# Strassen's seven products for the first two matrices of the second block's FFNs

## Chip, cores and metric

The kernel runs as one program on 1 core of one Trainium2 chip. The metric is device time in microseconds (us): the median of 3 runs of the kernel before is 2766.76 us (2765.35 to 2771.69).

## What is computed

The reference is a pair of two-layer transformer blocks on 256 tokens of width 1024, in float32. The change touches only the feed-forward networks (FFNs) of the second block. There are four of them: two layers `l`, two FFNs `f` in each.

```python
def swiglu_2(h, w_gate, w_up, w_down):
    return (jax.nn.silu(h @ w_gate) * (h @ w_up)) @ w_down

for l in range(DEPTH):                                   # DEPTH = 2
    h = rms_norm_2(x, norm_g[l, 0])
    x = x + 0.5 * swiglu_2(h, ffn_w_gate[l, 0], ffn_w_up[l, 0], ffn_w_down[l, 0])
    ...                                                  # attention
    h = rms_norm_2(x, norm_g[l, 2])
    x = x + 0.5 * swiglu_2(h, ffn_w_gate[l, 1], ffn_w_up[l, 1], ffn_w_down[l, 1])
```

Here `h` is 256 x 1024, `w_gate` and `w_up` are 1024 x 2816, and `w_down` is 2816 x 1024.

## The kernel before, in words

Every float32 operand is held as two parts, a rounded one (`h`, in tile `wh`) and what the rounding left out (`l`, in tile `wl`). `mm` (L432) multiplies two operands in three matmuls: high by high, high by low, low by high.

`Feed` (from L174) brings the weights. Its plan, made once by `all_weights` (L327), lists all weight blocks in the order in which TensorE uses them. `load` (L188) issues a 1 MB DMA on SP's queue for the next block (2048 columns of 128 partitions) as soon as a raw slot is free. `pump` (L202) splits the oldest raw block in pieces of 1024 columns: ScalarE copies the piece to `wh` with rounding (L220), and VectorE subtracts `wh` from the raw piece into `wl` (L221). Both of VectorE's inputs there lie in SBUF. At most `AHEAD` = 4 split pieces wait for TensorE. There are 3 raw and 3 split slots that all phases share, and 4 of each more while an FFN runs (`FFN_BUFS`). `take` (L231) hands a piece to TensorE's loop, `done` gives its slot back.

`ffn` (L560) goes over the 2816 middle columns in six chunks, five of 512 and one of 256. In a chunk `tokens` (L470) multiplies the tokens by the columns of `w_gate` (L610) and then by those of `w_up` (L611). Each has eight blocks of 128 rows and two tiles of 128 tokens, so 16 block products of three matmuls: 48 matmuls, 96 for both. ScalarE's Silu (L602) and VectorE's multiplication (L606) take the two results out of PSUM. Then `second` (L574) multiplies the chunk before by its rows of `w_down` (48 matmuls), TensorE transposes the chunk's result (L495), and ScalarE and VectorE split that as `gT` (L426, L427). Instructions run on each engine in the order in which they stand in its queue; GpSimd (POOL) has nearly nothing to do in the FFNs.

```python
            yield from self.tokens(xT, w1[:, f0:f0 + n], silu, ("lin", "lin"), ids)
            yield from self.tokens(xT, w3[:, f0:f0 + n], gate, ("tr" if nt == 2 else "lin", "lin"), ids)
            before = second(c - 1) if c else iter(())
```

Of the kernel before, what the change touches and what calls it, by code (L numbers as in the profile page):

```python
# [13 lines left out]
F32 = DT.float32  # L14
# [28 lines left out]
FFN_BUFS = (4, 4)  # L43
MOE_BUFS = (5, 4)
# [16 lines left out]
FFN_BANKS = {"acc": (0, 1, 2, 3), "lin": (4, 5), "tr": (6, 7)}  # L61
# [5 lines left out]
WIDE_CHUNKS = [(0, 512), (1024, 512), (2048, 384)]  # L67

# [84 lines left out]

class Feed:


    def __init__(self, nc, name):
        self.nc, self.name = nc, name
        self.free = ([], [])
        self.plan, self.raws, self.subs, self.plain = deque(), deque(), deque(), deque()  # L160
        self.live = deque()
        self.ahead = AHEAD
# [5 lines left out]
    def drop(self, phase):  # L168
# [19 lines left out]
    def load(self):  # L188

        if not self.plan:  # L190
            return False
        phase, src, k0, ks, split, heads = self.plan[0]
# [9 lines left out]
    def pump(self):  # L202
        nc = self.nc
        while True:
            moved = self.load()
            if self.raws and len(self.subs) < self.ahead:
# [3 lines left out]
                if slot:  # L210
# [13 lines left out]
                    if item[5] == kb:  # L224
                        self.raws.popleft()
                        self.free[0].append(rslot)
# [4 lines left out]
    def take(self, src):  # L231
# [3 lines left out]
        assert got.tensor.name == src.tensor.name and got.offset == src.offset and got.shape == src.shape  # L235
# [64 lines left out]
class Model:  # L300
# [28 lines left out]
    def all_weights(self):  # L329
        a, add = self.a, self.feed.add  # L330

        def ffn(phase, w1, w3, w2):
            n = len(FF_CHUNKS)
            down = lambda c: [w2[FF_CHUNKS[c][0]:sum(FF_CHUNKS[c]), :]]
            for c, (f0, m) in enumerate(FF_CHUNKS):
                add(phase, [w1[:, f0:f0 + m], w3[:, f0:f0 + m]])
# [95 lines left out]
    def mm(self, ps, lhs, rhs, start, stop):  # L432

        last = len(PASSES) - 1
        for i, (p, q) in enumerate(PASSES):
            self.nc.tensor.matmul(ps, lhs[p], rhs[q], start=start and i == 0, stop=stop and i == last)  # L436
# [123 lines left out]
    def ffn(self, pool, xT, w1, w3, w2, done, tiles=(0, 1), hook=None):  # L560
# [36 lines left out]
        for c, (f0, n) in enumerate(FF_CHUNKS):  # L597
# [12 lines left out]
            yield from self.tokens(xT, w1[:, f0:f0 + n], silu, ("lin", "lin"), ids)  # L610
            yield from self.tokens(xT, w3[:, f0:f0 + n], gate, ("tr" if nt == 2 else "lin", "lin"), ids)  # L611
# [1150 lines left out]
    def outer_norm(self, pool, gB):  # L1762

        nc = self.nc
        y = pool.tile([P, NT, D], F32, name="yout")
# [156 lines left out]
    def second_block(self):  # L1922
        nc, a = self.nc, self.a
        with self.tc.tile_pool(name="sb", bufs=1) as pool:
            half = lambda t, c0, n, ps: self.add_x(t, c0, n, ps, 0.5)
            col = lambda l, i: self.c1("norm_g_2", (l * 3 + i) * 8, 8)
            for l in range(L):
                for f in range(2):
                    with self.tc.tile_pool(name=f"f2_{l}{f}", bufs=1) as fp:
# [394 lines left out]
```

## Time and profile before

| | us |
|---|---|
| median of 3 runs (lowest, highest) | 2766.76 (2765.35, 2771.69) |
| the profiled execution's own time | 2769.47 |
| its span, first to last instruction | 2767.7 |
| TensorE busy in the span | 2708.2 |
| VectorE busy | 1909.6 |
| ScalarE busy | 1649.7 |
| GpSimd busy | 141.9 |
| first FFN of the second block, first matmul (1477.70) to the transposes after it (1663.77) | 186.07 |

The profile is of one execution. Busy time of TensorE includes the overlap of pipelined matmuls, so what a matmul costs is read from the distance between the starts of matmuls that follow each other and not from the length of one. The four FFNs lie at about 1478 to 1664, 1932 to 2115, 2122 to 2307 and 2576 to 2758 us of the span.

### The profile page before, as it was taken

What the parts mean: (1) busy time and instruction counts of PE and PEld (TensorE: products, weight loads), DVE (VectorE), ACT (ScalarE), POOL (GpSimd) and SP (SyncE); (2) the same over time, 40 slices, a digit from 0 to 9 for tenths busy, and PEclk for the clock granted to TensorE, in tenths of its full rate; (3) what the DMA queues carried; (4) which work ended last, traced back from release to release, by engine and by line L of the source; (5) the groups of instructions that cost most, each with busy time, mean ns of one, the idle gap of its engine ahead of it and who ended that gap; (6) DMA issues with size and microseconds to landing.
All of it is one profiled execution on the core that took longest, in us unless ns stands there. A gap on an engine that the chain in (4) does not pass through costs nothing. (4 is left out here: it accounts for less than half of the span.)

```text
span 2767.7 us, 38954 instructions
## 1 busy us (share of the span) xinstructions
PE 2708.2 (98%) x15206; PEld 2277.3 (82%) x15206; DVE 1909.6 (69%) x2618; ACT 1649.7 (60%) x2309; POOL 141.9 (5%) x183
## 2 busy tenths in 40 slices
PE   8999999999999999999989999999999999999998
PEld 7888888878888888888777888888888888988887
DVE  6565566668998998988876556776555446676554
ACT  6455455547887877777765446755444445674543
POOL 1220001310000000000000000010000000010000
PEclk9999999999999999999999999999999999999999
DMA  6327533337999999999966646446655546445651
GB/s 202 95 93 258 186 133 119 101 131 281 382 344 326 380 341 322 365 351 328 344 226 231 219 137 174 142 141 210 214 174 183 184 139 182 143 144 184 239 182 62
DMA packets 252646, 594.46 MB, mean 215 GB/s; under 512 B 26182, under 2 KB 62758, under 8 KB 252454
## 3 DMA queue, kind: packets, MB, share of 16 engines
q1 hardware_dynamic: 251206, 587.69, 61.1%
q0 software_dynamic: 1248, 4.20, 0.6%
q8 instruction: 122, 2.00, 0.3%
q14 instruction: 70, 0.57, 0.1%
HBM read 590.74 MB, written 1.10 MB: 214 GB/s over the span
## 5 line engine op out<-in xcount | busy, mean ns | idle before, releaser
L221 DVE TENSOR_TENSOR wl<-raw,wh 128x1024 fp32r<-128x1024 f32 (+2 forms) x1130 | 1314.3, 1186 | 596.9 <-ACT wh L220 583.6
L220 ACT ACTIVATE wh<-raw 128x1024 fp32r<-128x1024 f32 (+2 forms) x1130 | 1137.7, 1025 | 755.6 <-PE ps L436 708.1
L436 PE MATMUL ps<-wh,xT 128*128 128x512 f32 (+2 forms) x2944 | 919.2, 388 | 14.2 <-ACT xT L429 3.7
L436 PEld LDWEIGHTS ps<-wh,xT 128*128 128x128 f32 x2944 | 544.0, 190 | 136.7 <-DVE xT L430 7.5
L436 PE MATMUL ps<-wl,xT 128*128 128x512 f32 (+2 forms) x1472 | 563.9, 383 | 0.4 <-DVE wl L221 0.4
L436 PE MATMUL ps<-wh,gT 128*128 128x512 f32 x1584 | 500.3, 391 | 0.0
L436 PE MATMUL ps<-wh,xe 128*128 128x512 f32 (+1 forms) x1536 | 454.3, 373 | 0.0
L436 PEld LDWEIGHTS ps<-wh,gT 128*128 128x128 f32 x1584 | 297.3, 188 | 61.1
L436 PEld LDWEIGHTS ps<-wl,xT 128*128 128x128 f32 x1472 | 280.0, 190 | 53.8 <-DVE wl L221 2.1
L436 PEld LDWEIGHTS ps<-wh,xe 128*128 128x128 f32 x1536 | 284.5, 188 | 38.5
L436 PE MATMUL ps<-wl,gT 128*128 128x512 f32 x792 | 308.9, 391 | 0.9 <-DVE wl L221 0.8
L436 PE MATMUL ps<-wl,xe 128*128 128x512 f32 (+1 forms) x768 | 287.6, 375 | 2.7 <-DVE wl L221 2.4
L436 PE MATMUL ps<-xT,wh 128*128 128x256 f32 x960 | 177.9, 287 | 5.3 <-DVE z L845 2.7
L436 PEld LDWEIGHTS ps<-wl,gT 128*128 128x128 f32 x792 | 148.8, 188 | 32.6 <-DVE wl L221 2.3
L436 PEld LDWEIGHTS ps<-wl,xe 128*128 128x128 f32 x768 | 144.2, 188 | 27.3 <-DVE wl L221 7.0
L436 PEld LDWEIGHTS ps<-xT,wh 128*128 128x128 f32 x960 | 150.1, 192 | 7.8 <-ACT wh L220 2.8
L436 PE MATMUL ps<-xT,wl 128*128 128x256 f32 x480 | 135.8, 284 | 0.0
L436 PEld LDWEIGHTS ps<-xT,wl 128*128 128x128 f32 x480 | 92.0, 192 | 0.3 <-DVE wl L221 0.3
L1370 ACT ACTIVATE e<-e,mx 128x256 f32<-128x256 f32 (+1 forms) x160 | 76.0, 476 | 15.2 <-DVE mx L1368 14.8
L426 ACT ACTIVATE gT<-ps 128x512 fp32r<-128x512 f32 (+2 forms) x108 | 56.4, 553 | 30.1 <-PE ps L495 23.8
L503 ACT ACTIVATE junk<-x 128x512 bf16<-128x512 f32 x56 | 35.2, 628 | 63.3 <-DVE x L557 48.0
L427 DVE TENSOR_TENSOR gT<-ps,gT 128x512 fp32r<-128x512 f32 (+2 forms) x108 | 65.9, 639 | 0.6
(431 smaller groups left out, 2314.7 us busy)
## 6 DMA issues: line engine op xcount, KB each, us to landing
raw<-in_moe_w_dram SPq DMA_DIRECT2D x216, 1024.0 KB, 7.4
raw<-in_w_in_dram SPq DMA_DIRECT2D x50, 1024.0 KB, 5.2
raw<-in_moe_w_dram SPq DMA_DIRECT2D x64, 768.0 KB, 5.1
raw<-in_ffn_w_gate_dram SPq DMA_DIRECT2D x44, 1024.0 KB, 5.1
raw<-in_ffn_w_up_dram SPq DMA_DIRECT2D x44, 1024.0 KB, 5.5
raw<-in_ffn_w_down_dram SPq DMA_DIRECT2D x44, 1024.0 KB, 5.1
raw<-in_ffn_w_dram SPq DMA_DIRECT2D x33, 1024.0 KB, 5.2
raw<-in_w_gate_dram SPq DMA_DIRECT2D x24, 1024.0 KB, 5.1
```

What stands on the lines that cost most here:

```text
L220: nc.scalar.activation(ho, w, AF.Copy)
L221: nc.vector.tensor_tensor(lw, w, ho.bitcast(F32), op=ALU.subtract)
L426: nc.scalar.activation(h, src, AF.Copy)
L427: nc.vector.tensor_tensor(l, src, hf, op=ALU.subtract)
L436: self.nc.tensor.matmul(ps, lhs[p], rhs[q], start=start and i == 0, stop=stop and i == last)
L503: self.nc.scalar.activation(junk, self.x[:, t, h * 512:(h + 1) * 512], AF.Square, accum_out=ss[:, t, h:h + 1])
L1370: nc.scalar.activation(e[:, i], e[:, i], AF.Exp, bias=mx[:, i:i + 1], scale=-1.0, accum_out=sums[:, i:i + 1])
```

## The change

The two matrices of a chunk are seen as one 1024 x 1024 matrix of 2 x 2 blocks, each of 512 rows by 512 columns: `x1` and `x3` are the upper and the lower half of `w_gate`'s columns, `x0` and `x2` those of `w_up`'s. The tokens are 2 x 2 blocks too (128 tokens by 512 features). Strassen's scheme (in Winograd's form) makes the four results of seven block products instead of eight. For that four sums of weight blocks are needed (`t1` = x0 - x1, `t2` = x2 - t1, `t3` = x2 - x0, `t4` = x3 - t2), and four sums of token blocks, once for each FFN. The sums are made on GpSimd. It is done from the second chunk on; the first chunk is multiplied as before. A result now is a sum of products: three are added in PSUM, the others with copies (ScalarE) and additions (VectorE, and one on GpSimd).

```diff
+QUAD_BUFS = {(0, 0): (4, 4), (0, 1): (5, 4), (1, 0): (5, 4), (1, 1): (4, 4)}
-FFN_BANKS = {"acc": (0, 1, 2, 3), "lin": (4, 5), "tr": (6, 7)}
+FFN_BANKS = {"acc": (0, 1, 2, 3), "lin": (4, 5), "tr": (6, 7), "quad": (4, 5, 6, 7)}
...
+class Quad:
+    ORDER = ("x1", "t1", "t2", "x2", "t3", "x3", "t4")
+    LOADS = ("x1", "x0", "t1", "x2", "x3")
...
+    def sum(self, nc, out, a, b):
+        half = a.shape[1] // 2
+        for k in range(0, a.shape[1], half):
+            nc.gpsimd.tensor_tensor(out[:, k:k + half], a[:, k:k + half], b[:, k:k + half], op=ALU.subtract)
+
+    def derive(self, nc):
+        r = self.raw
+        if "t2" not in r and "x2" in r and "t1" in r and "x1" in self.split:
+            self.sum(nc, r["x1"], r["x2"], r["t1"])
+            r["t2"], self.slot["t2"] = r["x1"], self.slot["x1"]
+        elif "t3" not in r and "t2" in r:
+            self.sum(nc, r["x0"], r["x2"], r["x0"])
+            r["t3"], self.slot["t3"] = r["x0"], self.slot["x0"]
+        elif "t4" not in r and "t3" in r and "x3" in r and "t2" in self.split:
+            self.sum(nc, r["t2"], r["x3"], r["t2"])
+            r["t4"], self.slot["t4"] = r["t2"], self.slot["t2"]
...
+    def load_quad(self, phase, quad, name):
...
+        if name == "t1":
+            quad.sum(self.nc, raw, quad.raw["x0"], quad.raw["x1"])
+        else:
+            self.nc.sync.dma_start(raw, src.rearrange("(k p) n -> p k n", p=P))
...
+    def sums_T(self, pool, xT):
+        nc = self.nc
+        g = nc.gpsimd
+        full = [pool.tile([P, 4, S], F32, name=self.nm("full"), tag="gT0", bufs=2) for _ in range(2)]
+        for k, f in enumerate(full):
+            h, lo = [q[:, k * 4:k * 4 + 4, :].bitcast(F32) for q in xT.parts]
+            g.tensor_tensor(f, h, lo, op=ALU.add)
+        s = [pool.tile([P, 2, 4, P], F32, name=self.nm("sums"), tag="gT1", bufs=2) for _ in range(2)]
+        a = lambda t, k: full[k][:, :, t * P:(t + 1) * P]
+        g.tensor_tensor(s[0][:, 0], a(1, 0), a(1, 1), op=ALU.add)
+        g.tensor_tensor(s[0][:, 1], s[0][:, 0], a(0, 0), op=ALU.subtract)
+        g.tensor_tensor(s[1][:, 0], a(0, 0), a(1, 0), op=ALU.subtract)
+        g.tensor_tensor(s[1][:, 1], a(0, 1), s[0][:, 1], op=ALU.subtract)
+        parts = self.parts(pool, [P, 4, 4, P], "S")
+        for i in range(2):
+            self.put(parts, lambda q: q[:, 2 * i:2 * i + 2], s[i])
+        return parts
+
+    def quad(self, pool, quad, n, xT, sums, gs):
...
+        def gate(t):
+            g = (u2, u3)[t]
+            nc.vector.scalar_tensor_tensor(g, g, r[t], (p1, p5)[t], op0=ALU.mult, op1=ALU.mult)
+        def end_c11():
+            add(nc.vector, p1, C)
+            nc.scalar.activation(p1, p1, AF.Silu, scale=r[0])
+            gate(0)
+        def end_c22():
+            copy(u3, A)
+            nc.gpsimd.tensor_tensor(u3, u3, p5, op=ALU.add)
+        def end_c21():
+            nc.scalar.activation(p5, A, AF.Silu, scale=r[1])
+            gate(1)
...
+        plan = [
+            ("x1", A, xT.parts, own(0, 0), True, lambda: copy(p1, A)),
+            ("t1", B, sums, mixed(0), True, lambda: copy(p5, B)),
+            ("t2", A, sums, mixed(1), False, lambda: copy(u2, A)),
+            ("x2", B, sums, mixed(3), False, lambda: add(nc.vector, u2, B)),
+            ("t3", A, sums, mixed(2), False, end_c22),
+            ("x3", C, xT.parts, own(0, 4), True, end_c11),
+            ("t4", A, xT.parts, own(1, 4), False, end_c21),
+        ]
...
-            yield from self.tokens(xT, w1[:, f0:f0 + n], silu, ("lin", "lin"), ids)
-            yield from self.tokens(xT, w3[:, f0:f0 + n], gate, ("tr" if nt == 2 else "lin", "lin"), ids)
+            if c in quads:
+                yield from self.quad(pool, quads[c], n, xT, sums, gs)
+            else:
+                yield from self.tokens(xT, w1[:, f0:f0 + n], silu, ("lin", "lin"), ids)
+                if quads:
+                    sums = self.sums_T(pool, xT)
+                yield from self.tokens(xT, w3[:, f0:f0 + n], gate, ("tr" if nt == 2 else "lin", "lin"), ids)
```

How this moves instructions is seen in two places. The first is VectorE's queue in a middle chunk of the last FFN. Here is the kernel before, from a chunk's multiplications (L606) to the split of `gT` (L427); names with the same stem and another number are other buffers (`ps` lies in PSUM, all else in SBUF):

```order
L606 SCALAR_TENSOR_TENSOR g_27429<-ps_27365,rs_26922,sa_27355 128x512
L606 SCALAR_TENSOR_TENSOR g_27431<-ps_27366,rs_26922,sa_27357 128x512
L221 TENSOR_TENSOR wl_27434<-raw_27167,wh_27433 128x1024
L221 TENSOR_TENSOR wl_27452<-raw_27205,wh_27451 128x1024
L221 TENSOR_TENSOR wl_27468<-raw_27205,wh_27467 128x1024
L221 TENSOR_TENSOR wl_27486<-raw_27239,wh_27485 128x1024
L221 TENSOR_TENSOR wl_27518<-raw_27239,wh_27517 128x1024
L427 TENSOR_TENSOR gT_27502<-ps_27503,gT_27501 128x4x128
L427 TENSOR_TENSOR gT_27502<-ps_27510,gT_27501 128x4x128
```

In the changed kernel this is the stretch of a chunk that adds up the results (L302 is L221 of before, L681 the additions, L685 the multiplications, L519 is L427):

```order
L681 TENSOR_TENSOR g_27506<-ps_27502,g_27506 128x512
L302 TENSOR_TENSOR wl_27602<-raw_27297,wh_27601 128x1024
L302 TENSOR_TENSOR wl_27614<-raw_27280,wh_27613 128x1024
L302 TENSOR_TENSOR wl_27626<-raw_27280,wh_27625 128x1024
L302 TENSOR_TENSOR wl_27638<-raw_27359,wh_27637 128x1024
L681 TENSOR_TENSOR sa_27504<-ps_27503,sa_27504 128x512
L302 TENSOR_TENSOR wl_27651<-raw_27359,wh_27650 128x1024
L302 TENSOR_TENSOR wl_27663<-raw_27413,wh_27662 128x1024
L685 SCALAR_TENSOR_TENSOR g_27506<-g_27506,rs_27352,sa_27504 128x512
L685 SCALAR_TENSOR_TENSOR g_27507<-g_27507,rs_27352,sa_27505 128x512
```

A chunk of 512 columns had 12 splits on VectorE and now has 18, two additions out of PSUM are new, and the two multiplications now read both inputs from SBUF. The second place is GpSimd's queue, which had nothing in the chunks of an FFN. In the changed kernel one period of it, in the last FFN, is this (L174 are the halves of the weight sums, L694 is the addition of `end_c22`):

```order
L174 TENSOR_TENSOR raw_27581<-raw_27558,raw_27512 128x1024 x2
L694 TENSOR_TENSOR g_27507<-g_27507,sa_27505 128x512
L174 TENSOR_TENSOR raw_27558<-raw_27605,raw_27558 128x1024 x2
L174 TENSOR_TENSOR raw_27512<-raw_27605,raw_27581 128x1024 x2
L174 TENSOR_TENSOR raw_27512<-raw_27629,raw_27512 128x1024 x2
L174 TENSOR_TENSOR raw_27840<-raw_27817,raw_27771 128x1024 x2
```

The rows are `t1` of the next chunk, the addition for this chunk, then `t3`, `t2` and `t4` of the next, and `t1` of the one after: eight subtractions of 1024 columns for a chunk, and the addition ahead of three of the next chunk's sums.

## Rows read from the trace of the kernel before

**Rows 1.** The page: busy time by engine, the chain that ended last.

```profile
PE 2708.2 (98%) x15206; PEld 2277.3 (82%) x15206; DVE 1909.6 (69%) x2618; ACT 1649.7 (60%) x2309; POOL 141.9 (5%) x183
...
PE 36%; issue 7%; DVE 1%; DMA 1%; ACT 1%; ACTq 0%; POOLq 0%; POOL 0%; SPq 0%; DVEq 0%
```

**Rows 2.** Busy time by stretch: one middle chunk, first and last FFN.

```profile
core 0: us, PE busy (x) PEld busy (x) DVE busy (x) ACT busy (x) POOL busy (x), PEclk, DMA share, GB/s
...
1566.00:1600.00 34.00, 34.00 (x153) 27.75 (x152) 17.08 (x17) 14.96 (x16) 0.00 (x0) 1.00 0.55 187
...
1481.00:1666.00 185.00, 184.33 (x855) 150.93 (x855) 101.37 (x107) 84.04 (x98) 1.71 (x3) 0.98 0.58 198
...
2576.00:2761.00 185.00, 182.76 (x859) 150.68 (x857) 94.44 (x98) 81.06 (x95) 0.94 (x2) 1.00 0.46 158
```

**Rows 3.** Timeline of TensorE, first FFN: start, us, engine, line, operation, tiles, count.

```profile
1533.30 0.39 PE L436 MATMUL ps<-wl,xT 128*128 128x512 f32 x1
...
1554.99 0.40 PE L436 MATMUL ps<-wl,xT 128*128 128x512 f32 x1
...
1567.47 0.39 PE L436 MATMUL ps<-wl,xT 128*128 128x512 f32 x1
...
1635.69 0.28 PE L436 MATMUL ps<-wl,xT 128*128 128x256 f32 x1
...
1646.69 0.28 PE L436 MATMUL ps<-wl,xT 128*128 128x256 f32 x1
...
1646.92 0.40 PE L436 MATMUL ps<-wh,gT 128*128 128x512 f32 x1
...
1663.77 1.04 PE L535 MATMUL ps<-ident,x 128*128 128x128 f32 x8
```

**Rows 4.** Groups by form, VectorE, 1532 to 1634 us (count, busy, mean ns).

```profile
L221 DVE TENSOR_TENSOR wl<-raw,wh 128x1024 fp32r<-128x1024 f32 x36 | 44.1, 1226 | 48.4 <-ACT wh L220 48.3
L606 DVE SCALAR_TENSOR_TENSOR g<-ps,both,sa 128x512 f32<-128x512 f32 x6 | 4.2, 744 | 0.0
L427 DVE TENSOR_TENSOR gT<-ps,gT 128x512 fp32r<-128x512 f32 x6 | 3.8, 683 | 0.0
```

**Rows 5.** Groups by form, ScalarE, 1532 to 1634 us.

```profile
L220 ACT ACTIVATE wh<-raw 128x1024 fp32r<-128x1024 f32 x36 | 38.2, 1060 | 54.5 <-PE ps L436 52.7 <-DVE T L1889 1.7
L602 ACT ACTIVATE sa<-ps,both 128x512 f32<-128x512 f32 x6 | 4.1, 689 | 3.1 <-PE ps L436 3.1
L426 ACT ACTIVATE gT<-ps 128x512 fp32r<-128x512 f32 x6 | 3.2, 584 | 0.0
```

**Rows 6.** Groups by form, GpSimd, whole span.

```profile
L2215 POOL TENSOR_TENSOR y<-od,subg 128x512 f32<-128x512 f32 x4 | 5.2, 1297 | 0.3
...
L733 POOL TENSOR_TENSOR rp<-qraw,sincos 128x64 f32<-128x64 f32 x4 | 1.3, 318 | 0.0
```

**Rows 7.** Timelines of GpSimd and VectorE, attention, 1859 to 1872 us.

```profile
1860.95 2.55 POOL L2126 TENSOR_TENSOR merged<-merged,gate 128x512 f32<-128x512 f32 x2 [6.33 <-DVE gate L2125]
1867.61 3.53 POOL L2126 TENSOR_TENSOR merged<-merged,gate 128x512 f32<-128x512 f32 x2 [4.10 <-DVE gate L2125]
...
1861.29 0.69 DVE L2125 TENSOR_TENSOR gate<-ps,gate 128x512 f32<-128x512 f32 x1 [0.43 <-PE ps L436]
1862.44 2.14 DVE L221 TENSOR_TENSOR wl<-raw,wh 128x1024 fp32r<-128x1024 f32 x1 [0.46 <-ACT wh L220]
...
1868.43 1.55 DVE L221 TENSOR_TENSOR wl<-raw,wh 128x1024 fp32r<-128x1024 f32 x1 [0.30 <-ACT wh L220]
1870.90 1.32 DVE L221 TENSOR_TENSOR wl<-raw,wh 128x1024 fp32r<-128x1024 f32 x1 [0.92 <-ACT wh L220]
```

**Rows 8.** Granted clock (PEclk) around a stop of TensorE, first FFN's start.

```profile
1478.00:1488.00 10.00, 9.61 (x20) 5.40 (x19) 6.13 (x11) 7.31 (x11) 0.69 (x1) 0.51 0.98 340
1488.00:1498.00 10.00, 10.00 (x44) 8.03 (x43) 4.58 (x5) 3.18 (x3) 0.00 (x0) 0.98 0.94 340
...
1477.70 0.87 PE L436 MATMUL ps<-wh,xT 128*128 128x512 f32 x2 [1.81 <-ACT wh L220]
```

More of the change, by code (lines that the diff above doesn't have):

```diff
@@ L151, in backwards, with __init__, release @@
     return bass.AP(tensor=ap.tensor, offset=ap.offset + step * (n - 1), ap=dims)
+class Quad:
+    ORDER = ("x1", "t1", "t2", "x2", "t3", "x3", "t4")
+    LOADS = ("x1", "x0", "t1", "x2", "x3")
+    def __init__(self, w1, w3):
+        self.src = {"x1": w1[0:512, :], "x0": w3[0:512, :], "x3": w1[512:1024, :], "x2": w3[512:1024, :]}
+        self.raw, self.slot, self.split, self.gone = {}, {}, set(), set()
+    def sum(self, nc, out, a, b):
[14 more added lines that the diff above has]
+        else:
+            return False
+        return True
+    def release(self):
+        r, s = self.raw, self.split
+        over = {"t1": "t1" in s and "t2" in r, "x2": "x2" in s and "t3" in r, "t3": "t3" in s,
+                "x3": "x3" in s and "t4" in r, "t4": "t4" in s}
+        new = [n for n, o in over.items() if o and n not in self.gone]
+        self.gone.update(new)
+        return [self.slot[n] for n in new]
 class Feed:
@@ L205, in pump @@
             moved = self.load()
-            if self.raws and len(self.subs) < self.ahead:
+            for quad in self.quads:
+                moved |= quad.derive(nc)
+                self.free[0].extend(quad.release())
+            if self.quads and len(self.quads[0].split) == 7:
+                self.quads.pop(0)
+            if self.raws and self.raws[0][0] is None:
+                quad, n = self.raws[0][3]
+                self.raws[0][0] = quad.raw.get(n)
+            if self.raws and self.raws[0][0] is not None and len(self.subs) < self.ahead:
                 item = self.raws[0]
@@ L430, in put, with mm @@
             nc.vector.scalar_tensor_tensor(l, src, scale, hf, op0=ALU.mult, op1=ALU.subtract)
-    def mm(self, ps, lhs, rhs, start, stop):
+    def mm(self, ps, lhs, rhs, start, stop, reopens=False):
         last = len(PASSES) - 1
         for i, (p, q) in enumerate(PASSES):
-            self.nc.tensor.matmul(ps, lhs[p], rhs[q], start=start and i == 0, stop=stop and i == last)
+            self.nc.tensor.matmul(ps, lhs[p], rhs[q], start=start and i == 0, stop=stop and i == last,
+                                  skip_group_check=reopens)
     def mul(self, xT, sub, targets, last):
@@ L562, in ffn @@
+    def ffn(self, pool, xT, w1, w3, w2, done, tiles=(0, 1), hook=None, quads={}):
         nc = self.nc
```

68 lines of the change are left out of this document (60 added, 8 removed).

## The prediction

> **What bounds the kernel now.** I read the page first: TensorE is busy for 2708 of 2767.7 us and heads the chain that ended last, no other engine has over 69% [rows 1]. Then the stretches: in a middle chunk of an FFN TensorE works all 34 of 34 us, VectorE 17, ScalarE 15, GpSimd 0, at a granted clock of 1.00, and the first and the last FFN look the same (184 and 183 of 185 us) [rows 2]. So TensorE sets the pace there, and a matmul taken away is worth the distance between two starts. A chunk's first product steps from 1533.30 to 1554.99 in 31 groups of three matmuls, 0.70 us a group or 0.233 each; a whole chunk takes 1567.47 - 1533.30 = 34.17 us; in the last chunk, 256 columns wide, 31 groups take 1635.69 to 1646.69, 0.355 a group [rows 3]. But the change gives VectorE and GpSimd work in return, and the view to read next is what those two do to each other. That is seen only in the attention, where GpSimd works: a split on VectorE that takes 1.23 us by itself [rows 4] took 2.14 when it began inside two GpSimd multiplications, and it ended at 1864.58, 1.08 us after they did (1860.95 + 2.55 = 1863.50). In the next pair a split that began at 1868.43 took 1.55, and GpSimd's two instructions, 2.55 in the pair before, took 3.53: the second stood still until the split had ended (1869.98), and ended 1.16 us after that. A multiplication of VectorE that reads PSUM (1861.29) lies within GpSimd's work and takes its usual 0.69 [rows 7]. I read this as: an instruction of VectorE with two inputs in SBUF and one of GpSimd with two inputs in SBUF never run together; the one that comes later waits for the whole of the other. All splits are of the first kind, all new sums of the second.
>
> **What goes.** In a chunk 84 matmuls stand for 96, 12 fewer: 12 x 0.233 = 2.8 us in each of 16 full chunks, 12 x 0.118 = 1.4 in each of 4 last ones: 44.8 + 5.7 = 50.5 us of TensorE. A full chunk is then worth 34.17 - 2.8 = 31.4 us of TensorE.
>
> **What comes.** (1) Splits. A product has its own weights of 2048 columns, so a chunk has 7 x 2 = 14 pieces for 8, and with those of `w_down` 18 for 12. ScalarE: 6 x 1.06 us more, with four copies out of PSUM at about 0.69 some 9 us a chunk; it was idle for 54.5 of 102 us [rows 5], 18 us a chunk, which covers it. VectorE: 18 x 1.08, where 1.08 is what a split needs behind GpSimd [rows 7], makes 19.4 us. (2) The two multiplications now have both inputs in SBUF; at half a split's width I take 0.6 each, 1.2. (3) Two additions out of PSUM, and the two splits of `gT` that were there: 4 x 0.68 = 2.7 us by the nearest row (L427) [rows 4], beside which GpSimd may run. (4) GpSimd's eight subtractions of 1024 columns. No row has this width. Instructions with 512 columns take 1.297 and with 64 take 0.318 [rows 6], so a column costs 2.19 ns and 512 more cost 1.12: with the 1.16 of a queued one [rows 7] that gives 2.28; twice a lone one, 2.59, is the other bound. I take 2.3, by the row it is nearest to, since these will be queued: 8 x 2.3 = 18.4, and 1.2 for the addition: 19.6 us. The Trainium skill (GPSIMD Engine Reference, section 3.1) gives 4497 ns for an addition of 2048 columns, so 18.0 in place of 18.4; no run here shows that width.
>
> So a full chunk needs the excluded pair for 19.4 + 1.2 + 19.6 = 40.2 us, against 31.4 on TensorE and 34.2 before. **The work that hid VectorE is no longer enough cover**, and TensorE will wait for weights. It can't be evened out by working ahead, since only four pieces may be split ahead and `t4` waits for the split of `t2`.
>
> **The sum for one FFN.** VectorE: 8 splits of the first chunk, 56 + 7 of the products, 22 of `w_down`, 2 for the token sums = 95 x 1.08 = 102.6; multiplications 8 x 0.6 + 2 x 0.3 = 5.4. GpSimd: 32 subtractions and 2 token additions at 2.3 = 78.2; 8 narrow subtractions, 4 token sums and 4 additions at 1.16 = 18.6; 0.6 for the last addition. Together 205.4 us, of which 4 splits (4.3) are done before the FFN begins. Behind the last product's split TensorE still has that product (1.4) and `w_down`, 1663.77 - 1646.92 = 16.9 [rows 3], in which 6 splits and two multiplications (7.1) go on. So 205.4 - 4.3 + 18.3 - 7.1 = 212.3 us against 186.07, 26 more; four times, 105. Of VectorE's instructions that read PSUM (10 additions, 12 splits of `gT`, some 14 us an FFN) GpSimd's work covers a part; none to all is possible, and I count a third, 4.7, as added: 19 in all. 2769.5 + 105 + 19 = 2893 for the profiled execution; the median stands 2.7 us below it: **2890 us**, 4.5% slower.
>
> The bounds: with all of those covered and ten us more done ahead in each FFN, 4 x 16 = 64, 2831; with none covered and 2.59 for a subtraction (34 x 0.29 = 10 an FFN), 4 x (26 + 14 + 10) = 200, 2967.
>
> Edits at no cost: the DMAs carry the same bytes (eight more on SP's queue, from halving the last chunk's), at a busy share of 0.46 to 0.58 [rows 2]; were they late, raw slots would be the cause, of which the sum `t1` now holds one. The output tile shares a buffer with the token sums, which are long done by then. PSUM's four rotating banks can hold TensorE at a chunk's start until `gT` is split; the wait for weights is longer.
>
> **Rivals.** *Faster, the exclusion doesn't bite* (0.13). VectorE is idle for 48.4 of 102 us in the middle chunks, nearly all of it waiting for ScalarE [rows 4]; were the sums to fall in that time, TensorE would stay the bound and 50.5 us would be won, some 5 given back at the FFNs' starts: 2722. The deciding point is a subtraction's price: with 20.6 for VectorE and 1.2 for the addition, 31.4 leaves 9.6 us for eight, 1.2 each. Rows 6 have that for half the width, and [rows 7] show no overlap at all, in both orders.
>
> *A smaller loss* (0.12). The first chunk, the products with `w_down` and the gaps between phases take up more than I grant: 8 us an FFN, 2800.
>
> *Worse: stops of TensorE lower its clock* (0.11). At the first FFN's start TensorE stopped for 1.81 us, and in the 10 us from 1478 it was granted 0.51, the 1.2 GHz level, and did 20 matmuls where the next 10 us did 44 [rows 8]. A split that waits 2.3 us for GpSimd is such a stop. GpSimd's addition is one more: it waits for `t3`'s product and holds the next chunk's sums behind it. One stretch like that in each of 20 chunks, at 5 us, is 100: 2990. Against it, a slow TensorE lets the splits catch up. The Trainium skill (TensorE: Matmul & The Clock Gate, section "What's actually happening") calls the throttled state the default, released by activity; by that rule a TensorE busy for three quarters could lose its clock again and again; the trace agrees for this one stop, and no run here shows a long stretch at that share.
>
> *Nothing measurable* (0.02). The change does do what it says, 20 x 12 = 240 matmuls are gone from the queue, so gain and loss would have to cancel.
>
> **How the numbers follow.** The forecast has 0.62, and with the two other slow cases slower by over 0.2% (what a measurement of this kernel can tell from no change) has 0.85, within 0.2% 0.02, faster 0.13. The range leaves out the fast case, no change and the outer parts of the two slow rivals: 2790 to 3000.
>
> **What would show it.** Right: in the middle chunks TensorE is busy for about three quarters, with idle time ended by L302 (`wl`); splits have a mean well over 1.23 us and GpSimd's subtractions well over 2.3, because both contain waits; a chunk takes 40 to 43 us. Wrong: splits stay at 1.23 beside GpSimd's work, or a subtraction takes near 1.2 us, and a chunk takes 31 to 32 us; or TensorE's clock falls in the chunks, and the loss is nearer to 220 us.

## The result and the profile after

The changed kernel takes 2947.56 us (median of 4 runs, 2944.71 to 2950.75), the kernel before beside it 2767.71 (4 runs, 2765.35 to 2771.69): a ratio of 1.0649 with a 95% interval of 1.0630 to 1.0667, 180 us slower. The forecast was 2890, with a range of 2790 to 3000 and 0.85 for slower.

The page of the changed kernel, with the rows that answer to [rows 1] (busy time of each engine, the chain that ended last):

```profile
PE 2712.0 (92%) x14966; PEld 2240.0 (76%) x14966; DVE 2317.9 (79%) x2774; ACT 1797.8 (61%) x2505; POOL 680.6 (23%) x387
...
PE 25%; DVE 12%; issue 6%; POOL 3%; ACT 2%; DMA 2%; SPq 0%; ACTq 0%; POOLq 0%; DVEq 0%
```

The 240 matmuls are gone (15206 to 14966), yet TensorE was busy no less (2708.2 to 2712.0). VectorE rose by 408 us and now stands in the chain with 12% instead of 1%; GpSimd rose from 142 to 681.

Where in the program? A chunk ends with the transposes of its result (L588), so their starts mark the chunks. The timeline of TensorE in the second FFN (start, us, engine, line, operation):

```profile
2041.74 1.03 PE L588 MATMUL ps<-ident,g 128*128 128x128 f32 x8
...
2085.84 1.04 PE L588 MATMUL ps<-ident,g 128*128 128x128 f32 x8
```

From one to the next is 44.1 us. The table was made in this way for both kernels from their timelines; "to the first" is the distance from the last transposes of the FFN before (for the first FFN, of the phase before) to the first of this one, so it holds all that lies between, the start and the ordinary first chunk.

| FFN | before: to the first, then chunks 2 to 6 | after | more |
|---|---|---|---|
| 1 | 90.3; 33.7 34.2 34.2 34.2 17.7 | 97.7; 44.0 43.9 44.2 39.1 17.3 | 41.9 |
| 2 | 296.9; 33.8 34.3 34.3 34.3 17.7 | 308.1; 42.1 44.1 47.3 38.2 16.3 | 44.8 |
| 3 | 37.8; 33.9 34.3 34.3 34.3 17.7 | 48.4; 41.9 44.3 47.6 38.1 16.3 | 44.3 |
| 4 | 296.9; 33.8 34.3 34.3 34.3 17.7 | 312.0; 39.0 45.1 45.5 39.1 17.3 | 46.7 |

The four sums make 177.7 us, so the loss lies in these FFNs: 44 us in the four stretches to the first transposes (7.4 + 11.2 + 10.6 + 15.1) and 133 in the chunks. Chunks 2 to 4 take 39 to 48 us, chunk 5 some 38 to 39, and the half chunk is a little faster than before.

Busy time by stretch, changed kernel: three full chunks of the second FFN and its half chunk (columns as in [rows 2]).

```profile
1999.67:2041.74 42.07, 32.69 (x138) 24.73 (x139) 40.91 (x25) 21.89 (x25) 25.42 (x10) 1.00 0.45 150
2041.74:2085.84 44.10, 33.74 (x141) 24.91 (x140) 40.54 (x25) 22.70 (x26) 26.16 (x10) 1.00 0.43 143
2085.84:2133.14 47.30, 34.84 (x141) 26.26 (x140) 40.47 (x25) 22.72 (x26) 26.30 (x10) 0.96 0.36 122
...
2171.39:2187.73 16.34, 16.34 (x117) 15.32 (x116) 15.83 (x16) 12.53 (x18) 5.21 (x3) 1.00 0.22 68
```

In a full chunk VectorE shows 40 to 41 us of work and GpSimd 26, together 66 in 42 to 47: both counts hold the time for which an instruction stands blocked by the other engine. TensorE has 33 to 35, three quarters. In the half chunk TensorE is busy throughout.

Groups by form, changed kernel: VectorE from 1990 to 2450 us, then GpSimd over the whole span (count, busy, mean ns, idle before).

```profile
L302 DVE TENSOR_TENSOR wl<-raw,wh 128x1024 fp32r<-128x1024 f32 x186 | 341.7, 1878 | 37.5 <-ACT wh L301 37.1
```

```profile
L174 POOL TENSOR_TENSOR raw<-raw,raw 128x1024 f32<-128x1024 f32 x128 | 392.8, 3084 | 236.8 <-DVE wl L302 219.0 <-DMA raw<-in_ffn_w_up_dram 17.9
```

A split has a mean of 1878 ns, where it had 1226 [rows 4], with the same form and line of code. VectorE's idle time behind ScalarE, 48.4 us of 102 before, is 37.5 of 460.

What TensorE waited for, changed kernel, from 1485 us to the end (total us, times, longest):

```profile
PE ps L528 <- DVE wl L302: 127.1, 106, 4.1
PE ps L528 <- DVE gT L519: 22.2, 8, 4.0
PE ps L528 <- ACT wh L301: 18.1, 3, 7.1
```

In the kernel before, from 1479 us on, the same view has this row for `wl` (L221) and none for the other two:

```profile
PE ps L436 <- DVE wl L221: 0.4, 1, 0.4
```

So 167.4 us of new stops stand against 50.5 us saved, 117 net. And TensorE's busy time, 3.8 us more with 50.5 us of matmuls fewer, says that the others took some 54 longer. The clock is about half of that: the mean granted clock is 0.982 over 2942.9 us and was 0.991 over 2767.7, so 53.0 and 24.9 us of full speed are missing, 28 more.

One of those stops, in the fourth FFN, shows how the pieces hang together. The timeline of GpSimd, of VectorE and of TensorE, changed kernel (in brackets the idle time before and what ended it):

```profile
2832.30 2.41 POOL L174 TENSOR_TENSOR raw<-raw,raw 128x1024 f32<-128x1024 f32 x1 [8.43 <-DVE wl L302]
2835.87 3.32 POOL L174 TENSOR_TENSOR raw<-raw,raw 128x1024 f32<-128x1024 f32 x1 [1.16 <-DVE wl L302]
```

```profile
2819.20 2.47 DVE L302 TENSOR_TENSOR wl<-raw,wh 128x1024 fp32r<-128x1024 f32 x1 [0.87 <-ACT wh L301]
2821.87 3.08 DVE L302 TENSOR_TENSOR wl<-raw,wh 128x1024 fp32r<-128x1024 f32 x1 [0.20 <-ACT wh L301]
2824.87 1.27 DVE L519 TENSOR_TENSOR gT<-ps,gT 128x512 fp32r<-128x512 f32 x2
2831.00 1.22 DVE L302 TENSOR_TENSOR wl<-raw,wh 128x1024 fp32r<-128x1024 f32 x1 [4.85 <-ACT wh L301]
2833.33 10.35 DVE L302 TENSOR_TENSOR wl<-raw,wh 128x1024 fp32r<-128x1024 f32 x6 [1.11 <-ACT wh L301]
```

```profile
2825.60 0.79 PE L528 MATMUL ps<-wh,S 128*128 128x512 f32 x1 [3.99 <-DVE gT L519]
```

The split that began at 2821.87 stands behind GpSimd and takes 3.08 us instead of 1.2. Behind it in VectorE's order is the split of `gT` (L519), which frees the PSUM bank that the next product's result is to use; TensorE stops for 3.99 us. The windows around it:

```profile
2820.00:2823.00 3.00, 1.62 (x12) 1.21 (x10) 2.80 (x2) 2.03 (x3) 3.00 (x2) 1.00 0.14 57
2823.00:2831.00 8.00, 5.40 (x13) 4.28 (x14) 3.15 (x4) 1.06 (x1) 0.87 (x1) 0.57 0.43 133
2831.00:2838.00 7.00, 6.51 (x29) 5.03 (x28) 5.89 (x4) 5.57 (x8) 4.54 (x2) 1.00 0.00 0
```

The second window begins inside the stop; its mean clock is 0.57, and it has 13 matmuls where the next 7 us have 29. Here are the 5 us right behind this stop, then the start of the matmul behind the next stop for `gT`, one of 3.63 us, and the 5 us behind that:

```profile
2825.60:2830.60 5.00, 5.00 (x12) 3.93 (x13) 0.55 (x1) 0.69 (x1) 0.00 (x0) 0.50 0.69 213
...
2873.59 0.50 PE L528 MATMUL ps<-wh,S 128*128 128x512 f32 x1 [3.63 <-DVE gT L519]
...
2873.59:2878.59 5.00, 5.00 (x22) 4.16 (x23) 4.43 (x3) 3.02 (x4) 3.85 (x2) 1.00 0.33 101
```

Behind the first TensorE is granted 0.50, the 1.2 GHz level, and does 12 matmuls; behind the second 1.00, and it does 22. Of the eight stops for `gT` (3.98, 3.07, 2.99, 0.83, 2.96, 0.78, 3.99 and 3.63 us, in order of time) five have 0.50 to 0.66 in the 5 us behind them; the two short ones and the last have 1.00. So the length of a stop alone does not tell whether the clock falls. From 2823 to 2831 VectorE works 3.15 of 8 us and GpSimd 0.87: GpSimd's next sum waited 8.43 us for a split, and the split for ScalarE. That time, unlike a stop for a split, is lost to the excluded pair too.

### The profile page after: what moved, and what is told of

Same layout as the page of the kernel before. It is cut to its first block, busy times and chain, and to the rows that moved or that the text cites. A ratio compares the mean times of both kernels' runs of the same rounds, so it can differ in the third digit from the quotient of the medians.

```text
span 2942.9 us, 39264 instructions
## 1 busy us (share of the span) xinstructions
PE 2712.0 (92%) x14966; PEld 2240.0 (76%) x14966; DVE 2317.9 (79%) x2774; ACT 1797.8 (61%) x2505; POOL 680.6 (23%) x387
## 4 chain that ended last, share of the span: by engine, by line
PE 25%; DVE 12%; issue 6%; POOL 3%; ACT 2%; DMA 2%; SPq 0%; ACTq 0%; POOLq 0%; DVEq 0%
PE ps L528 22%; DVE wl L302 10%; POOL raw L174 2%; ACT wh L301 1%; PE ps L2267 1%; PE ps L588 1%; DMA raw<-in_ffn_w_up_dram 1%; PE ps L1546 1%; DMA narows<-rpbscr 1%; PE ps L2433 0%; POOL full L660 0%; DVE g L685 0%; PE ps L2170 0%; DMA raw<-in_ffn_w_gate_dram 0%; PE ps L2173 0%
## 5 line engine op out<-in xcount | busy, mean ns | idle before, releaser
L302 DVE TENSOR_TENSOR wl<-raw,wh 128x1024 fp32r<-128x1024 f32 (+3 forms) x1238 | 1666.6, 1379 | 344.1 <-ACT wh L301 328.0
L301 ACT ACTIVATE wh<-raw 128x1024 fp32r<-128x1024 f32 (+3 forms) x1238 | 1244.7, 1027 | 673.4 <-PE ps L528 604.5
L528 PE MATMUL ps<-wh,xT 128*128 128x512 f32 (+2 forms) x2144 | 703.8, 399 | 38.2 <-ACT wh L301 20.0
L174 POOL TENSOR_TENSOR raw<-raw,raw 128x1024 f32<-128x1024 f32 (+1 forms) x160 | 457.9, 2877 | 287.0 <-DVE wl L302 258.1
L528 PEld LDWEIGHTS ps<-wh,xT 128*128 128x128 f32 x2144 | 407.1, 194 | 136.1 <-ACT wh L301 21.7
L528 PE MATMUL ps<-wl,xT 128*128 128x512 f32 (+2 forms) x1072 | 426.6, 398 | 58.7 <-DVE wl L302 58.5
L528 PEld LDWEIGHTS ps<-wl,xT 128*128 128x128 f32 x1072 | 208.1, 194 | 118.0 <-DVE wl L302 82.1
L528 PE MATMUL ps<-wh,S 128*128 128x512 f32 (+1 forms) x640 | 193.2, 380 | 19.9 <-DVE gT L519 18.2
L528 PE MATMUL ps<-wl,S 128*128 128x512 f32 (+1 forms) x320 | 125.3, 392 | 49.8 <-DVE wl L302 49.7
L528 PEld LDWEIGHTS ps<-wh,S 128*128 128x128 f32 x640 | 119.2, 193 | 44.1 <-DVE gT L519 20.7
```

The costliest lines, as they stand in the source:

```text
L174: nc.gpsimd.tensor_tensor(out[:, k:k + half], a[:, k:k + half], b[:, k:k + half], op=ALU.subtract)
L301: nc.scalar.activation(ho, w, AF.Copy)
L302: nc.vector.tensor_tensor(lw, w, ho.bitcast(F32), op=ALU.subtract)
```

## The experiments

Each diff is against the changed kernel unless another is named. Two questions were open: is it really that VectorE and GpSimd exclude each other, and not the number of instructions, the waits or the DMAs; and why is the loss 178 us where the sum had 124.

**The sums left out, and written without reading.** The first kernel leaves out the weight sums, the second puts two memsets of the same piece in the place of each.

```diff
-            nc.gpsimd.tensor_tensor(out[:, k:k + half], a[:, k:k + half], b[:, k:k + half], op=ALU.subtract)
+            pass
...
         if name == "t1":
-            quad.sum(self.nc, raw, quad.raw["x0"], quad.raw["x1"])
-        else:
+        if True:
```

> The four sums of weight blocks on GpSimd are left out (t1 is filled by a second load of x0, the other three keep what lies in their slot); products, splits, additions and token sums stay. Theory A (GpSimd's sums and VectorE's splits exclude each other): without the sums TensorE is the bound again, a full chunk takes 32 to 34 us in place of 44, and the time is 2735 to 2770 us. Rival B (VectorE's own additional work, 18 splits for 12 and the additions, is too much): a chunk stays at 38 us or more, over 2850 us.

```diff
-            nc.gpsimd.tensor_tensor(out[:, k:k + half], a[:, k:k + half], b[:, k:k + half], op=ALU.subtract)
+            nc.gpsimd.memset(out[:, k:k + half], 0.5)
+            nc.gpsimd.memset(out[:, k:k + half], 0.25)
```

> Each half of a weight sum is replaced by two memsets of the same 128x1024 piece: GpSimd still writes the slot between load and split, in the same place of its queue, and is busy for about as long (two memsets of about 1 us for 2.3 us), but reads nothing from SBUF. Theory A (exclusion of instructions that read two inputs from SBUF): VectorE's splits go back to 1.23 us and the time is within 25 us of the run without sums. Rival C (the chain load, sum, split and GpSimd's order of work cost the time, whatever GpSimd does there): over 2880 us.

Measured: 2748.84 us (ratio 0.9925, interval 0.9898 to 0.9952) without sums, and 2746.9 (0.9923, 0.9895 to 0.995) with memsets. VectorE's splits from 1500 to 2960 us, without sums:

```profile
L300 DVE TENSOR_TENSOR wl<-raw,wh 128x1024 fp32r<-128x1024 f32 x502 | 625.3, 1267 | 185.7 <-ACT wh L299 183.3 <-PE ps L526 1.2
```

With memsets, VectorE's splits, GpSimd's memsets over the whole span, and one middle chunk:

```profile
L303 DVE TENSOR_TENSOR wl<-raw,wh 128x1024 fp32r<-128x1024 f32 x502 | 622.9, 1262 | 188.7 <-ACT wh L302 187.0 <-PE ps L529 0.6
```

```profile
L175 POOL MEMSET raw<- 128x1024 f32 x128 | 121.0, 961 | 3.0
```

```profile
2203.50:2237.10 33.60, 31.47 (x142) 25.69 (x141) 25.86 (x24) 22.55 (x26) 15.95 (x17) 1.00 0.51 173
```

GpSimd works for 16 of 33.6 us in that chunk, with the same order and the same tiles, and a split takes 1262 ns: an instruction of GpSimd that reads nothing does not hold the splits up. Two memsets are 1.92 us, a subtraction by itself is 2.35, so GpSimd's own time is nearly the same. So the 200 us between these two kernels and the changed one are the price of subtractions that read SBUF, not of GpSimd being in the chain. Without sums the full chunks of FFNs 2 to 4 take 30.7 to 33.5 us, so the 31.4 worked out for TensorE can be had, and the stretches to the first transposes (92.5, 299.2, 39.6, 303.8) are only 1.8 to 6.9 us longer than before.

**The same subtractions without Strassen.** The kernel before, with twelve subtractions on GpSimd in each chunk from the second on, in tiles of their own that nobody waits for.

```diff
+        dummy = [pool.tile([P, 1024], F32, name=self.nm("dummy"), tag=f"dummy{i}") for i in range(3 if subs else 0)]
...
+            if c:
+                for i in range(subs):
+                    nc.gpsimd.tensor_tensor(dummy[2], dummy[0], dummy[1], op=ALU.subtract)
```

> The kernel before, with eight products, plus 12 subtractions of 1024 columns on GpSimd for each chunk from the second on; they read and write tiles of their own, nothing waits for them but GpSimd's queue. Theory A: an FFN needs 60 x 2.3 + 66 x 1.08 = 209 us of the excluded pair against 186 us on TensorE, and splits stand behind whole subtractions: 2850 to 2930 us, splits with a mean well over 2 us. Without an exclusion: within 10 us of 2768, splits at 1.23 us.

Measured: 2919.43 us, 1.0559 (1.0541 to 1.0576). A stretch as long as a middle chunk, and the two groups by form from 1991 to 2160 us, VectorE and GpSimd:

```profile
2080.00:2120.10 40.10, 37.27 (x153) 27.05 (x152) 40.10 (x17) 14.97 (x17) 39.16 (x13) 1.00 0.47 157
```

```profile
L221 DVE TENSOR_TENSOR wl<-raw,wh 128x1024 fp32r<-128x1024 f32 x49 | 151.2, 3141 | 7.4 <-ACT wh L220 7.1
```

```profile
L604 POOL TENSOR_TENSOR dummy<-dummy,dummy 128x1024 f32<-128x1024 f32 x53 | 169.4, 3197 | 4.1
```

Nothing in this kernel waits for a result of these subtractions, and still chunks 4 and 5 of FFNs 2 to 4 go from 34.3 to 40.1 us (some chunks of the first FFN take longer still, up to 58.4, which was not looked into), with VectorE shown as busy for all of it and GpSimd for 39. Twelve splits and twelve subtractions in 40.1 us are 3.34 us a pair, close to the 1.08 and 2.3 of the forecast together. The exclusion is shown, and it needs nothing of the change but the subtractions. The Trainium skill (SBUF — State Buffer, section "SBUF: two separate sides") states it for VectorE's instructions with two SBUF inputs only against an instruction of GpSimd that reads SBUF; the memsets and the subtractions here agree with both halves of that.

**One PSUM bank fewer.** The products' banks no longer take in the bank 7 of the transposes.

```diff
-FFN_BANKS = {"acc": (0, 1, 2, 3), "lin": (4, 5), "tr": (6, 7), "quad": (4, 5, 6, 7)}
+FFN_BANKS = {"acc": (0, 1, 2, 3), "lin": (4, 5), "tr": (6, 7), "quad": (4, 5, 6)}
```

> The products of a chunk turn through three PSUM banks (4, 5, 6) in place of four (4, 5, 6, 7), so that the first product of a chunk no longer needs a bank that holds the transposes of the chunk before. Theory D (the stops of about 4 us at a chunk's start, and the half clock behind them, are a cost of their own): 30 to 60 us less, 2890 to 2915 us. If the exclusion alone sets the pace (A in its pure form), the stop only moves to the next wait for a split: within 10 us of 2947.

Measured: 2926.73 us, 1.0575 (1.0542 to 1.0608), 21 us less than the changed kernel: less than the 30 to 60 us that were expected if the bank stops are a cost of their own, and more than the 10 if the stop only moves. What TensorE waits for from 1485 us on has no `gT` row left, and the wait for `wl` is longer, 140.7 us for 127.1. A middle chunk of the third FFN:

```profile
2272.50:2315.00 42.50, 33.12 (x142) 25.12 (x141) 40.76 (x25) 22.96 (x26) 27.24 (x10) 1.00 0.44 148
```

```profile
PE ps L528 <- DVE wl L302: 140.7, 112, 4.5
PE ps L528 <- ACT wh L301: 17.9, 3, 6.8
```

Chunks 2 to 4 of FFNs 2 and 3 are now all alike, 42.1 to 42.5 us (44.1 to 47.6 in chunks 3 and 4 before this edit). The stops for `gT` gave up 22.2 us, 13.6 of that came back as waits for `wl`, and the remaining 12 or so go with the slow matmuls behind the stops: by the granted clock the 5 us behind five of them lack some 11 us of full speed (an estimate from those five windows), and the chunk that had 0.96 and 47.3 us has a clock of 1.00 here. What is left, 42.3, is 2 us more than the 40.2 that the forecast had for the excluded pair; it had up to 2.7 beside that for the four instructions of VectorE that read PSUM, and how much of them GpSimd's work covers was not measured.

**The sums on VectorE.** The same eight subtractions a chunk, on the busier engine of the two; then the same with three banks.

```diff
-            nc.gpsimd.tensor_tensor(out[:, k:k + half], a[:, k:k + half], b[:, k:k + half], op=ALU.subtract)
+            nc.vector.tensor_tensor(out[:, k:k + half], a[:, k:k + half], b[:, k:k + half], op=ALU.subtract)
```

> The four sums of weight blocks are made on VectorE in place of GpSimd. Theory A: nothing is excluded any more except for the one addition; VectorE needs 26 instructions of 1.14 us, two multiplications and four instructions that read PSUM, 33 to 34 us a full chunk, and a chunk takes 34 to 37 us: 2770 to 2830 us. Rival B (VectorE is overloaded by itself): 18 us of GpSimd's work a chunk are put on the fullest engine, slower than 2947 us.

> The sums on VectorE, and three rotating PSUM banks in place of four. Theory A with D (bank stops add about 20 us): 2827 - 20, 2800 to 2815 us; VectorE's 33 to 34 us a full chunk is then the bound, so no gain on the kernel before. If the bank stop only moves: within 8 us of 2827.

Measured: 2826.86 us, 1.0206 (1.0174 to 1.0239), and with three banks 2800.2, 1.0131 (1.0114 to 1.0148). VectorE with the sums on it and four banks, 1500 to 2960 us (the splits) and whole span (the sums), then a middle chunk of the kernel with three banks:

```profile
L302 DVE TENSOR_TENSOR wl<-raw,wh 128x1024 fp32r<-128x1024 f32 x505 | 618.8, 1249 | 105.6 <-ACT wh L301 104.8 <-DMA narows<-rpbscr 0.5
```

```profile
L174 DVE TENSOR_TENSOR raw<-raw,raw 128x1024 f32<-128x1024 f32 x128 | 164.8, 1324 | 1.0 <-DMA raw<-in_ffn_w_up_dram 0.4
```

```profile
2200.00:2234.00 34.00, 32.17 (x142) 25.36 (x141) 34.00 (x33) 22.95 (x27) 5.22 (x1) 1.00 0.53 186
```

Giving work to the busier engine of the two made the kernel 121 us faster. A subtraction costs VectorE 1.3 us; on GpSimd it cost the pair 2.35 and more. But now VectorE is busy for the whole of the 34.0 us, about a chunk (GpSimd's one addition, put at 1.2 us, shows 5.22 there: it still stands behind VectorE). VectorE is the bound, 2.6 us above the 31.4 of TensorE, and nothing is won against the 34.3 of before.

**Fewer of the chunks.** If VectorE is full in a seven-product chunk and half idle in an ordinary one, alternating them lets it work ahead. With the sums on VectorE, and with them on GpSimd, both with three banks (the edits above and this one):

```diff
-                if c and phase in QUADS:
+                if c % 2 and phase in QUADS:
...
-                if quads:
+                if quads and c == 0:
```

> As the run with the sums on VectorE and three banks, but seven products only in every other chunk (the second, the fourth and the last). Theory A: VectorE has 17 us of idle time in the chunks between and 33 to 34 us of work in a chunk of seven products, so TensorE stays near its bound: 7 us an FFN are taken from TensorE and some 3 to 5 given back at the FFN's start (sums of the token blocks): 2755 to 2775 us. Rival (each chunk of seven products costs on its own, whatever lies between): half way from 2768 to the run with all chunks.

> The same alternation with the sums on GpSimd, as in the change. Theory A: a chunk of seven products needs 40 us of the excluded pair and a chunk between 14 of 34; what can be spread over both is limited by the raw slots and by four pieces ahead, so a chunk of seven products takes 36 to 42 us and the time is 2785 to 2850 us, clearly over the same kernel with sums on VectorE. If GpSimd's part doesn't matter once the chunks alternate: equal to that kernel.

Measured: 2782.8 us, 1.0059 (1.0042 to 1.0076) on VectorE, 2814.68, 1.0182 (1.0165 to 1.0199) on GpSimd. The first misses its 2755 to 2775 us and lies at the rival's number, half way from 2768 to 2800. The chunks speak against the rival: they did what they should, 30.2 to 32.7 us for a seven-product chunk and 34.3 for an ordinary one; the whole loss is in the four stretches to the first transposes, 8.3 to 14.0 us each. On GpSimd, with the same slack around them, the seven-product chunks of FFNs 2 and 3 take 34.0 to 34.2 us: less than the 36 to 42 expected, but no gain over an ordinary one, and the four stretches are 8.5 to 13.5 us longer. So the starts cost much the same whichever engine makes the weight sums, and in both kernels a seven-product chunk follows right behind the first. Moving it off (the edits of the first kernel, with this one in place of the alternation):

```diff
-                if c and phase in QUADS:
+                if c in (2, 4, 5) and phase in QUADS:
```

> Sums on VectorE, three banks, seven products in the third, the fifth and the last chunk only, so that the first chunk has no chunk of seven products behind it. Theory A and E (in the run with alternation, chunks gained 2.8 to 3 us as forecast, and all of the loss lies at the FFNs' starts): TensorE's gain is 3 + 3 + 1.4 us an FFN, 30 us in all; if half of the 8 to 14 us at a start was the second chunk's sums beside the first, 2755 to 2765 us; if all of it is the sums of the token blocks, 2770 to 2785 us.

Measured: 2758.83 us (7 runs, 2754.87 to 2762.76), 0.9966 (0.9955 to 0.9978), some 9 us faster than the kernel before and 189 faster than the change. A seven-product chunk:

```profile
2164.00:2195.30 31.30, 31.30 (x142) 25.59 (x141) 27.49 (x27) 22.63 (x26) 4.78 (x1) 1.00 0.66 235
```

TensorE works all of the 31.3 us, and VectorE 27.5 with 27 instructions, where the stretch with all chunks had 33: part of its work was done in the chunk before. The stretches to the first transposes are 94.0, 297.2, 39.6 and 307.5, so 3.7, 0.3, 1.8 and 10.6 longer than before, 16 us in all where the alternation had 40: more than half of what the starts cost came with the seven-product chunk right behind the first. In the last stretch TensorE stops for 4.48 us for `xT` and for 1.89 us for a maximum in the attention, with half clock behind both; why it stops there was not looked for.

**What costs at the start?** The changed kernel at the second FFN's start: the timelines of GpSimd and of ScalarE, and two windows.

```profile
1971.65 0.72 POOL L615 TENSOR_TENSOR rs<-rs,mhalf 128x2 f32<-128x2 f32 x1 [5.50 <-DVE rs L614]
1972.36 5.76 POOL L174 TENSOR_TENSOR raw<-raw,raw 128x1024 f32<-128x1024 f32 x2
1978.09 2.39 POOL L660 TENSOR_TENSOR full<-xT,xT 128x1024 f32<-128x1024 f32 x1
1980.55 1.29 POOL L663 TENSOR_TENSOR sums<-full,full 128x512 f32<-128x512 f32 x1
...
1988.81 2.35 POOL L174 TENSOR_TENSOR raw<-raw,raw 128x1024 f32<-128x1024 f32 x1
```

```profile
1984.37 1.06 ACT L518 ACTIVATE S<-sums 128x1024 fp32r<-128x1024 f32 x1 [6.86 <-POOL sums L664]
1988.88 1.06 ACT L518 ACTIVATE S<-sums 128x1024 fp32r<-128x1024 f32 x1 [3.46 <-POOL sums L666]
1989.84 3.88 ACT L301 ACTIVATE wh<-raw 128x1024 fp32r<-128x1024 f32 x4
```

```profile
1971.65:1991.20 19.55, 13.32 (x56) 10.45 (x56) 5.52 (x5) 7.46 (x9) 19.43 (x10) 0.91 0.51 196
1991.20:1999.67 8.47, 6.13 (x14) 3.91 (x14) 8.47 (x7) 3.58 (x4) 5.08 (x2) 0.60 0.39 124
```

GpSimd works for 19.4 us without a gap, on weight sums and token sums one behind the other; ScalarE waits for the token sums twice with four weight splits behind it, and TensorE stops for 6.2 us for `wh` and then runs at 0.60. Two orders were tried. In the first the norm's small power on GpSimd (L615), which TensorE's results are scaled with, is put ahead of all token sums, by a tiny addition that reads it; once on the kernel with the third, fifth and last chunk, and once on the changed kernel:

```diff
             h, lo = [q[:, k * 4:k * 4 + 4, :].bitcast(F32) for q in xT.parts]
+            g.tensor_tensor(f[:, 0, 0:NT], xT.rstd, xT.rstd, op=ALU.add)
             g.tensor_tensor(f, h, lo, op=ALU.add)
```

> The same, and the sums of the token blocks wait for the norm's factors (a tiny addition that reads them writes into their tile first), so that GpSimd makes the power for the norm (L615) before and not behind them. Theory E2 (the late norm holds the first chunk's results in PSUM and stops TensorE at every FFN's start): 15 to 30 us less than the run before it, 2735 to 2755 us, under the kernel before. If the order on GpSimd at the start doesn't matter: equal to the run before it.

> The change as it is, with the norm's power ahead of the sums of the token blocks on GpSimd. Theory E2: 10 to 30 us less than 2947, 2915 to 2937 us. If the excluded pair is behind anyway at the start, the time is caught up nowhere and nothing is won: within 8 us of 2947.

Measured: 2765.03 us (11 runs, 2758.16 to 2770.49), 0.999 (0.9978 to 1.0001), and 2956.32, 1.068 (1.0663 to 1.0696). Both miss what they were to show: no gain, but some 6 us more on the one and 9 on the other, where the intervals just touch or overlap. The test is a narrow one, though: in three of the changed kernel's four starts only one token sum stood ahead of the power anyway (above, L615 at 1971.65 runs before the other five), and in the first FFN, where all six did, the stretch to the first transposes grew from 97.7 to 101.6 us. So an earlier power gains nothing here, and the token sums that now wait for it come later.

In the second the splits of the token sums are written behind the first chunk's second projection, so that they no longer stand ahead of its weights in ScalarE's order:

```diff
-        parts = self.parts(pool, [P, 4, 4, P], "S")
-        for i in range(2):
-            self.put(parts, lambda q: q[:, 2 * i:2 * i + 2], s[i])
-        return parts
+        return s
...
                 yield from self.tokens(xT, w3[:, f0:f0 + n], gate, ("tr" if nt == 2 else "lin", "lin"), ids)
+                if quads:
+                    sums = self.split_S(pool, sums)
```

> The changed kernel with one thing put elsewhere in the program: the two splits of the token sums into S (L518, L519) are written behind the first chunk's second projection instead of ahead of it. The sums themselves stay on GpSimd where they were, no work is left out or added. At three of the changed kernel's four FFN starts ScalarE stands 6.9 to 8.3 us and then 1.9 to 3.5 us for GpSimd's token sums, with the splits of the first chunk's second projection queued behind it, and TensorE then stops for 4.8, 6.2 and 7.1 us for `wh` of L301. Theory Q (the queue of ScalarE): these stops go, and with them the half-clock stretch behind one of them; the distance from the last FFN's transposes to the first of the next falls from 308.1, 48.4 and 312.0 to between 298 and 304, 39 and 44, 300 and 306; the first FFN, which has no such stop, keeps about 97; the chunks stay as they were. Median 2915 to 2932 us. Theory X (the excluded pair's work at the start, whichever queue it stands in): the work is the same, the stops only come later, at the first seven-product chunk, and the median is within 8 us of 2947.6.

Measured: 2953.46 us (5 runs, 2950.4 to 2958.26), 1.0671 (1.0651 to 1.069), 6 us from the changed kernel: theory X. Timeline of TensorE, second FFN's start:

```profile
1997.30 0.79 PE L528 MATMUL ps<-wh,S 128*128 128x512 f32 x1 [5.33 <-ACT wh L301]
2003.11 0.80 PE L528 MATMUL ps<-wl,S 128*128 128x512 f32 x1 [5.02 <-DVE wl L302]
```

The stop of 6.2 us in the first chunk is gone, and two of 5.3 and 5.0 stand at the first product with token sums. The queue only chose the place; the work at the start is what costs. With the weight sums left out the same stretches were 1.8 to 6.9 us longer than before, 13 in all, with them 7.4 to 15.1, 44 in all, so most of it is the weight sums. With these on VectorE and three banks it stayed at 7.6 to 13.1 (97.9, 305.4, 45.6 and 310.0). The exclusion is not gone from the start in that kernel, since the token sums are still made on GpSimd; one of 512 columns has a mean of 1962 ns there for the 1.29 us above:

```profile
L663 POOL TENSOR_TENSOR sums<-full,full 128x512 f32<-128x512 f32 x4 | 7.8, 1962 | 0.3
```

Which wait ends last at the start was not settled.

## Why the prediction was right, and where it was short

**The exclusion, the ground of the whole forecast, is shown.** It was read from two pairs of instructions in the attention [rows 7], and no subtraction of this width had been seen. It held: by the memsets, by the kernel before with idle subtractions, and by the 121 us that came from giving VectorE more to do.

**A subtraction's price** was put at 2.3 us between 2.28 and 2.59. The least of the 128 took 2.35, and ones that nothing delayed 2.35 to 2.41: 0.05 to 0.11 more, under 1 us a chunk. The Trainium skill (GPSIMD Engine Reference, section 3.1) gives 4497 ns for 2048 columns; two of these here are 4.7 to 4.8, a little over it.

**The chunk** was to take 40 to 43 us, bounded by the pair with 40.2. With the bank stops taken out chunks 2 to 4 take 42.1 to 42.5 (FFNs 2 and 3); in the changed kernel itself they take 39.0 to 47.6. What was to show it was there: TensorE busy for 33.7 of 44.1 us, its idle time ended by `wl` of L302, splits at 1878 ns and subtractions at 3084.

**TensorE's saving** of 2.8 us a chunk is real: 31.3 us in the kernel that lets TensorE be the bound, for 34.2.

**The step that was short** is the one among the edits at no cost: "PSUM's four rotating banks can hold TensorE at a chunk's start until `gT` is split; the wait for weights is longer". The two waits do not lie beside each other; the split of `gT` stands in VectorE's order behind splits that are blocked themselves. There were eight stops, 22.2 us, with half clock behind five of them: taking one bank away gave back 21 us. The rival on the clock had the mechanism in part: a stop can be followed by half clock, but not in each of the 20 chunks. In the 42.5 us chunk with three banks seven stops at splits, of 0.6 to 1.7 us, left the clock at 1.00, though TensorE was busy there for only 78%; in the changed kernel a stop of 3.99 us was followed by 0.50 and one of 3.63 us by 1.00. What decides between them was not settled. The Trainium skill (TensorE: Matmul & The Clock Gate, section "What's actually happening") calls the throttled state the default, released by activity; the prediction took from it that the clock could fall again and again at such a share, and this chunk doesn't show that.

**The second term** is the sum for one FFN, 217.0 us with the third of the PSUM instructions for a measured 186.07 + 44.4 = 230.5. It added all work of the pair as if it were done without gaps from the FFN's start on. Within the chunks that is nearly so: even in the half chunk, where TensorE is busy for all 16.34 us, VectorE is for 15.83. The gaps are at the bank stops (from 2823 to 2831 us VectorE works 3.15 and GpSimd 0.87 of 8 us). With these gone a middle chunk still takes 42.3 us for the 40.2, and the start, for whose stops the sum has no term and where GpSimd works 19.4 us in a row with ScalarE and TensorE waiting behind it, came to 44 us over the four FFNs. Of the 54 us missed the banks hold 21; the remaining 33 lie at the starts and in the chunks, and were not told apart further. That the time, 58 us over the forecast, still fell within the range is in part luck: the room up to 2967 was worked out from subtractions of 2.59 us and PSUM instructions that nothing covers, and what took it up were bank stops and starts.

The rivals: "the exclusion doesn't bite" is refuted, and the two kernels without the reading subtractions show that it would have been 2747 to 2749, not 2722: what separates them, 25 us, is in part 9.0 and 8.5 us of stops for `gT` that were priced at nothing there, too, and in part the starts, 13 and 16 us longer where 5 were granted.

## What to carry to other kernels

Moving work from a full engine to an idle one is no gain if the two can't run together: before giving GpSimd an operation with SBUF inputs, count what VectorE reads twice from SBUF in that stretch, and add the two instead of taking the larger. A trade of TensorE time for VectorE time pays only where VectorE has a slack of its own and can work ahead into it, so place it in the chunks that have one (the third, the fifth and the last here, 9 us faster than before) and not right behind a phase's start. A buffer that is freed by an instruction behind delayed ones is delayed with them, and a stop of some microseconds can cost more than its length: five of the eight bank stops here had half clock behind them.

## What the runs showed of the hardware

- GpSimd's memset of 128x1024 float32, which writes only, took 0.96 us and did not lengthen a split on VectorE (1262 ns beside 16 us of memsets a chunk).
- The exclusion needs no dependence: subtractions in tiles of their own took 3.2 us each beside splits that took 3.1, one pair in 3.34 us, for 2.35 and 1.23 by themselves. Engines' busy time then counts the waiting: 40.1 and 39.2 us in a chunk of 40.1.
- A stop of 3.99 us on TensorE was followed by 5 us at a granted clock of 0.50, one of 3.63 us by 5 us at 1.00, both with 1.00 ahead of them; a chunk in which TensorE was busy 33.1 of 42.5 us, with seven stops of 0.6 to 1.7 us, kept 1.00.
